# Threshold search of the 896- and 1024-key blocks begun only with group A, in smaller intervals there

## The chip, the cores and the metric

One core of a Trainium2 chip runs the program. The metric is the device time of one execution in microseconds (us). The engines are named as in the profile: PE is TensorE (PEld its weight loads), DVE VectorE, ACT ScalarE, POOL GpSimd, SP SyncE. Each has its own queue of instructions, in a fixed order.

## What is computed

One decoder layer on 1024 tokens of width 1024. Its first part, the token mixer, has two groups of heads: group A (8 heads of sparse attention, in which each query sees only the 256 keys with the highest score of a small indexer) and group B (4 heads of differential attention). Cross-attention and a gated feed-forward part follow. What matters here is the selection in group A:

```python
logits = jnp.einsum('bqhd,bsd->bqhs', qib, k_idx)
score = jnp.einsum('bqh,bqhs->bqs', wib, jax.nn.relu(logits)).astype(jnp.float32)
score = jnp.where(causal[None], score, -jnp.inf)
_, idx = lax.top_k(score, topk)            # topk = 256
...
s = jnp.where(valid[:, :, None, :], s, -jnp.inf)
p = jax.nn.softmax(s, axis=-1).astype(v.dtype)
```

## The kernel before

Tokens are tiled in eight blocks of 128 queries; by causality block i sees (i+1)*128 keys, so block 6 has 896 keys and block 7 has 1024. The stages run one after the other: the input projections with the indexer's scores (phase 0 of the search), group B (phase 1, four heads of eight units; the loop over `s` with `b_qt`, `b_s`, `b_comb`, `b_t`, `b_av`), group A (phase 2, eight blocks of eight heads; the loop with `a_t`, `a_s`, `a_av`), then the output projection of the second half, cross-attention and the feed-forward part. After block 3's last head the output projection of the first half (`wout_unit`) runs between the units of A.

The selection is not a sort. For each query row of blocks 2 to 7 a threshold is searched bit by bit, 32 iterations (`topk_iter`, L541), and then a mask is made of it (`topk_mask`, L587). Four groups of blocks are searched: blocks 2 and 3, then block 6, by ScalarE ("act"); blocks 4 and 5, then block 7, by VectorE ("dve"). An "act" iteration is one Sign with a running sum over the block's scores (L553, ScalarE) and two small VectorE instructions that make the next threshold (L555, L557); the next iteration's Sign reads that threshold. A "dve" iteration is one count (L565, VectorE) and two small instructions (L567 and L568, or L570 and L571); its first iteration has a copy on ScalarE (L562) and its sixteenth converts the scores (L580, L581). A mask is a row of VectorE instructions over the whole block (L594 to L607). Group A may not begin a block before its mask is there: `a_s` calls `topk_finish`, which issues what is still missing.

When an iteration is issued is set by hand, in virtual microseconds. After each piece of work the program calls `tick(us)`; while a queue's head is due, `us` is added to what it is owed, and whenever `PACE` of that queue is owed one iteration is issued, behind the last ScalarE and VectorE instruction of the work around it. A queue's head is due once the scores of its last block are there (`scored`). `PACE` has one pair (act, dve) for each phase:

```python
PACE = [dict(...) for x in '4,6:7,12:4,4.5'.split(':')]   # phases 0, 1, 2
```

The places of the instructions on each engine come from a scheduler that works from the program's order. Other lines that the steps below touch: in B, L774 is VectorE's masked reduction of a score row, L776 ScalarE's exp, L748 and L682 ScalarE's copies of transposed queries and probabilities, L726 VectorE's split of transposed keys, L907 a copy for the memory's keys, L797 TensorE's product with the values; in A, L1018 is the reduction, L1019 the exp, L682 the copy, L1036 the product, L1061 and L1062 ScalarE's and VectorE's part of the mixed output's split.

Of the kernel before, what the change touches and what calls it, by code (L numbers as in the profile page):

```python
# [44 lines left out]
def hybrid_layer(ctx, tc, I, out):  # L45
    nc = tc.nc
    pe, act, dve, pool, sp = nc.tensor, nc.scalar, nc.vector, nc.gpsimd, nc.sync
# [562 lines left out]
    topk_q = {"act": [], "dve": []}  # L610
# [3 lines left out]
    owed = {"act": 0.0, "dve": 0.0}  # L614
    last = {}
    scored = [1]

    PACE = [dict(zip(("act", "dve"), [float(y) for y in x.split(",")])) for x in '4,6:7,12:4,4.5'.split(':')]
    phase = [0]

    def tick(us):

        pace = PACE[phase[0]]
        for on in ("act", "dve"):
            if not topk_q[on] or topk_q[on][0][0] > scored[0]:
                continue
            owed[on] += us
            while owed[on] >= pace[on] and topk_q[on] and topk_q[on][0][0] <= scored[0]:
                owed[on] -= pace[on]
                with tc.issue_after(last["act"].ins), tc.issue_after(last["dve"].ins):  # L630
                    topk_q[on].pop(0)[1]()
# [202 lines left out]
    for c in range(2, 5):  # L834
        for t in range(NT):
            X = proj_mm(c, t)
            if c == 4 and t == 3:
                b_load_k(0)
            if c == 4 and t >= 4:
                b_k(0, (t - 4) // 2, 4 * (t % 2))  # L840
            if t == 7:
                W.free(8)
            W.pump(1 if t < 7 else 2)
            for _ in range(2):
                if idxq:
                    idxq.pop(0)()
            tick(5.2)
            if store:
                store()
            if c == 4 and t >= 6:  # L850
                b_load_q(t - 6)
            store = proj_post(c, t, X)
# [78 lines left out]
    def mem_unit(p):  # L931
        w_, c, t = mem_units.pop(0)
        X = mem_evac(t, p)
        if t == 1:
            W.free(4)
            if (w_, c) == ("xv", 1):
                W.free(2)
        if w_ == "xk":
            memk_post(c, t, X)
            mem_late.append(lambda: memk_tr(c, t, X))  # L940
        else:
            sp.dma_start(vx_d[t * P:(t + 1) * P, c * 512:(c + 1) * 512], X)
        tick(5.2)
# [6 lines left out]
    for s in range(-4, NB):  # L950
# [28 lines left out]
        if ok(s):  # L979
            b_av(s)  # L980
            W.pump(1)
            tick(0.8 + 0.85 * (i + 1))
# [753 lines left out]
```

## Time and profile before

| | us |
|---|---|
| median of 3 runs | 1676.73 (1675.79 to 1676.85) |
| profiled execution, its own time | 1677.18 |
| its span, first to last instruction | 1675.4 |
| PE busy | 1572.9 (94%) |
| DVE busy | 1222.3 (73%) |
| ACT busy | 804.1 (48%) |
| POOL busy | 641.2 (38%) |

The shares are means over stages that differ. Group B's first reduction starts at 281.1 us and group A's at 480.5; A's last block ends before 710. In these 430 us the search stands beside attention, and the rows below are taken from there. A busy share says what an engine did; what held it up is read from its waits, each put down to the instruction that came last.

### The profile page before, as it was taken

How to read it: one execution, taken by the hardware profiler on the slowest of the kernel's cores; microseconds unless marked ns; L12 is line 12 of the kernel's file. 1: busy time of each engine (PE TensorE's matmuls, PEld its weight loads, DVE VectorE, ACT ScalarE, POOL GpSimd, SP SyncE). 2: the span in 40 equal slices, each digit the busy share in tenths (PEclk: the TensorE clock that was granted, in tenths of full speed). 3: DMA queues.
4: the chain of work that ended last, by engine and by line, in shares of the span. 5: the costliest groups of instructions: out<-in, count | busy, mean ns of one | idle time of the engine just before them, and what ended most of it. 6: DMA issues, size and time to landing. Idle time of an engine off the chain costs nothing.

```text
span 1675.4 us, 22263 instructions
## 1 busy us (share of the span) xinstructions
PE 1572.9 (94%) x7596; PEld 1273.4 (76%) x7596; DVE 1222.3 (73%) x2356; ACT 804.1 (48%) x1696; POOL 641.2 (38%) x888
## 2 busy tenths in 40 slices
PE   8899987878888999999999997999999999999999
PEld 7788765666657888977777785888888777788887
DVE  5736998886778876346555369998899999865554
ACT  6545575576777445527443175432333333343432
POOL 2736656223361122031101013556666666651121
PEclk9999998989999999999999998999999999999999
DMA  8321236212120132153203021455555555799812
GB/s 283 99 83 47 77 126 212 75 51 74 49 66 27 51 101 77 45 175 115 101 1 113 26 89 63 163 170 188 177 176 178 183 187 184 253 357 379 307 51 76
DMA packets 112162, 220.06 MB, mean 131 GB/s; under 512 B 18480, under 2 KB 38448, under 8 KB 112048
## 3 DMA queue, kind: packets, MB, share of 16 engines
q1 hardware_dynamic: 91072, 148.37, 26.5%
q0 software_dynamic: 18384, 61.36, 10.3%
q10 hardware_dynamic: 2592, 8.91, 1.4%
q8 instruction: 60, 0.98, 0.2%
q14 instruction: 54, 0.44, 0.1%
HBM read 160.92 MB, written 57.67 MB: 130 GB/s over the span
## 4 chain that ended last, share of the span: by engine, by line
PE 57%; DVE 23%; DMA 7%; ACT 6%; issue 4%; POOL 3%; SPq 0%; ACTq 0%; DVEq 0%; POOLq 0%
PE acc L308 9%; PE acc L310 9%; PE acc L309 9%; PE big L309 3%; PE big L310 3%; PE big L308 3%; DVE wp L204 3%; PE acc L1036 2%; DVE jk L565 2%; PE trp L308 2%; PE trp L310 2%; PE trp L309 2%; PE trp L691 2%; DMA raw<-in_w_ffn_in_dram 2%; PE acc L885 2%
## 5 line engine op out<-in xcount | busy, mean ns | idle before, releaser
L204 DVE TENSOR_TENSOR wp<-raw,wp 128x512 fp32r<-128x512 f32 (+1 forms) x184 | 183.4, 1006 | 28.3 <-ACT wp L201 17.2
L201 ACT CAST wp<-raw 128x512 fp32r<-128x512 f32 (+1 forms) x184 | 108.4, 615 | 176.6 <-DVE raw L227 113.6
L1600 DVE TENSOR_TENSOR wp<-fo,wp 128x1024 fp32r<-128x1024 f32 x77 | 104.2, 1370 | 75.3 <-ACT wp L1599 71.6
L1549 POOL TENSOR_TENSOR fs<-fs,fs 128x512 f32<-128x512 f32 x88 | 127.6, 1450 | 63.4 <-DMA fs<-u_d 49.0
L1599 ACT CAST wp<-fo 128x1024 fp32r<-128x1024 f32 x77 | 79.8, 1049 | 107.7 <-PE big L310 46.1
L308 PE MATMUL acc<-wp,xh 128*128 128x512 f32 (+1 forms) x272 | 110.1, 407 | 10.0 <-ACT X L646 10.0
L310 PE MATMUL acc<-wp,xl 128*128 128x512 f32 (+1 forms) x272 | 109.5, 403 | 0.0
L309 PE MATMUL acc<-wp,xh 128*128 128x512 f32 (+1 forms) x272 | 109.2, 403 | 0.0
L553 ACT ACTIVATE mb<-sc,cand 128x384 bf16<-128x384 f32 (+1 forms) x96 | 75.4, 786 | 39.6 <-DVE cand L557 35.8
L203 POOL TENSOR_SCALAR wp<-raw 128x512 fp32r<-128x512 f32 (+1 forms) x36 | 24.9, 698 | 177.0 <-DVE rst L110 63.5
L682 ACT COPY pt<-trp 128x512 f32<-128x512 f32 (+3 forms) x144 | 66.3, 476 | 41.2 <-PE trp L691 40.6
L1036 PEld LDWEIGHTS acc<-va_t,pt 128*128 128x128 f32 x576 | 75.1, 196 | 9.6 <-ACT pt L682 7.6
L1036 PE MATMUL acc<-va_t,pt 128*128 128x65 f32 x576 | 77.8, 274 | 4.0 <-ACT pt L682 3.8
L1646 POOL TENSOR_TENSOR hr<-hr,r 128x512 f32<-128x512 f32 x16 | 26.8, 1686 | 115.6 <-DMA fo<-ws_d 58.4
L308 PEld LDWEIGHTS acc<-wp,xh 128*128 128x128 f32 x272 | 52.7, 194 | 23.5 <-ACT X L646 12.2
L1018 DVE CUSTOM_DVE_ANT_0 ea<-big,mb,ra 128x384 f32<-128x384 f32 (+5 forms) x48 | 45.4, 946 | 27.5 <-PE trp L691 24.4
L1497 ACT ACTIVATE fc<-fc 128x1024 f32<-128x1024 f32 x22 | 23.4, 1062 | 84.8 <-DVE fc L1496 84.8
L204 POOL TENSOR_TENSOR wp<-raw,wp 128x512 fp32r<-128x512 f32 x36 | 47.5, 1336 | 42.1 <-ACT wp L201 41.8
L774 DVE CUSTOM_DVE_ANT_0 e<-big,tri,rqk 128x1024 f32<-128x1024 f32 (+7 forms) x64 | 50.4, 812 | 16.9 <-PE big L767 14.6
L1494 ACT ACTIVATE fc<-fa,cw 128x1024 f32<-128x1024 f32 x22 | 27.4, 1245 | 71.5 <-DVE fa L1453 71.5
L1019 ACT ACTIVATE ea<-ea,sta 128x128 f32<-128x128 f32 (+7 forms) x64 | 49.5, 777 | 24.9 <-DVE sta L1018 23.0
L310 PEld LDWEIGHTS acc<-wp,xl 128*128 128x128 f32 x272 | 52.4, 193 | 11.5
(422 smaller groups left out, 5133.3 us busy)
## 6 DMA issues: line engine op xcount, KB each, us to landing
raw<-in_w_ffn_in_dram SPq DMA_DIRECT2D x44, 512.0 KB, 4.0
fs<-in_w_ffn_out_dram POOLq DMA_DIRECT2D x44, 256.0 KB, 3.5
ws_d<-fs POOLq DMA_DIRECT2D x44, 256.0 KB, 2.3
fs<-u_d POOLq DMA_DIRECT2D x44, 256.0 KB, 3.8
us_d<-fs POOLq DMA_DIRECT2D x44, 256.0 KB, 3.5
fo<-us_d SPq DMA_DIRECT2D x44, 256.0 KB, 5.4
fo<-ws_d SPq DMA_DIRECT2D x44, 256.0 KB, 5.4
u_d<-fg POOLq DMA_DIRECT2D x21, 512.0 KB, 3.7
```

The costliest lines, as they stand in the source:

```text
L201: act.copy(pg[:, 0, :n], src)
L204: (dve if el == "d" else pool).tensor_tensor(pg[:, 1, :n], src, pg[:, 0, :n].bitcast(F32), op=OP.subtract)
L308: pe.matmul(o, lhsT=lh, rhs=rh, start=start, stop=False)
L309: pe.matmul(o, lhsT=lh, rhs=rl, start=False, stop=False)
L310: pe.matmul(o, lhsT=ll, rhs=rh, start=False, stop=stop)
L553: act.activation(mb[i], sc[i], AF.Sign, bias=cf[:, j:j + 1], scale=-1.0, accum_out=cnt[:, j:j + 1])
L682: act.copy(dst, src)
L774: dve.tensor_tensor_reduce(e[:, :n], Ss[c][:, :n], tri[:, T - n:], rqk[h // 2][:, i, 2 * (h % 2) + c:2 * (h % 2) + c + 1], 3.0e38, OP.add, ...
L1036: pe.matmul(acc[:, hh * 65:hh * 65 + 65], lhsT=pt, rhs=va_t[:, kt, :], start=kt == 0, stop=kt == i)
L1549: pool.tensor_tensor(o, p, q, op=op)
L1599: act.copy(hi, raw)
L1600: dve.tensor_tensor(lo, raw, hi.bitcast(F32), op=OP.subtract)
```

## The change

In phases 0 and 1 an iteration is now due only while the queue's head belongs to a block up to 5: the searches of block 6 (act) and block 7 (dve) are not begun before group A. The intervals change too: in phase 1 that of "dve" from 12 to 10, in phase 2 from 4 and 4.5 to 2.6 and 3.2.

```diff
@@ -615,17 +615,21 @@
     last = {}
     scored = [1]
 
-    PACE = [dict(zip(("act", "dve"), [float(y) for y in x.split(",")])) for x in '4,6:7,12:4,4.5'.split(':')]
+    PACE = [dict(zip(("act", "dve"), [float(y) for y in x.split(",")])) for x in '4,6:7,10:2.6,3.2'.split(':')]
     phase = [0]
+
+    def due(on):
+
+        return bool(topk_q[on]) and topk_q[on][0][0] <= (scored[0] if phase[0] == 2 else min(scored[0], 5))
 
     def tick(us):
 
         pace = PACE[phase[0]]
         for on in ("act", "dve"):
-            if not topk_q[on] or topk_q[on][0][0] > scored[0]:
+            if not due(on):
                 continue
             owed[on] += us
-            while owed[on] >= pace[on] and topk_q[on] and topk_q[on][0][0] <= scored[0]:
+            while owed[on] >= pace[on] and due(on):
                 owed[on] -= pace[on]
                 with tc.issue_after(last["act"].ins), tc.issue_after(last["dve"].ins):
                     topk_q[on].pop(0)[1]()
```

Three places show what this moves; the added lines shift the line numbers behind L618 by four. The first is ScalarE in group B, where head 2 begins (`e` with 1024 columns is block 7's exp). Before:

```order
L776 ACTIVATE e_3254,st_3240<-e_3254,st_3240 128x1024
L553 ACTIVATE mb_940,ccnt_526<-sc_941,cand_522 128x896
L776 ACTIVATE e_3331,st_3325<-e_3331,st_3325 128x256
L907 COPY kt_3264<-trp_3259 128x512
L894 ACTIVATE sq_3269<-X_3267 128x512
L776 ACTIVATE e_3331,st_3325<-e_3331,st_3325 128x256
L798 ACTIVATE ob_2719<-acc_3097,st_3120 128x128
L748 CAST qbs_3317<-trp_3314 128x256
L553 ACTIVATE mb_940,ccnt_526<-sc_941,cand_522 128x896
L682 COPY pt_3323<-trp_3319 128x384
```

And with the change:

```order
L780 ACTIVATE e_3250,st_3236<-e_3250,st_3236 128x1024
L780 ACTIVATE e_3321,st_3315<-e_3321,st_3315 128x256
L911 COPY kt_3260<-trp_3255 128x512
L898 ACTIVATE sq_3265<-X_3263 128x512
L780 ACTIVATE e_3321,st_3315<-e_3321,st_3315 128x256
L802 ACTIVATE ob_2719<-acc_3097,st_3120 128x128
L752 CAST qbs_3307<-trp_3304 128x256
L686 COPY pt_3313<-trp_3309 128x384
```

The two Signs are gone; exp, copies and casts follow each other.

The second is ScalarE in group A, the fifth to seventh head of block 4 (640 keys). Before:

```order
L1019 ACTIVATE ea_5643<-ea_5643,sta_5490 128x640
L1061 CAST mx_5554<-trp_5556 128x512
L682 COPY pt_5576<-trp_5571 128x512
L1047 ACTIVATE sq_5798<-ob_2719 128x512
L682 COPY pt_5580<-trp_5578 128x128
L1019 ACTIVATE ea_5687<-ea_5687,sta_5490 128x640
L1061 CAST mx_5554<-trp_5595 128x512
L682 COPY pt_5632<-trp_5627 128x512
L682 COPY pt_5636<-trp_5634 128x128
L1019 ACTIVATE ea_5740<-ea_5740,sta_5490 128x640
```

And with the change:

```order
L1023 ACTIVATE ea_5633<-ea_5633,sta_5469 128x640
L1065 CAST mx_5539<-trp_5541 128x512
L686 COPY pt_5564<-trp_5559 128x512
L553 ACTIVATE mb_940,ccnt_526<-sc_941,cand_522 128x896 x3
L686 COPY pt_5568<-trp_5566 128x128
L553 ACTIVATE mb_940,ccnt_526<-sc_941,cand_522 128x896
L1023 ACTIVATE ea_5683<-ea_5683,sta_5469 128x640
L1065 CAST mx_5539<-trp_5583 128x512
L553 ACTIVATE mb_940,ccnt_526<-sc_941,cand_522 128x896
L686 COPY pt_5622<-trp_5617 128x512
L686 COPY pt_5626<-trp_5624 128x128
L1023 ACTIVATE ea_5743<-ea_5743,sta_5469 128x640
```

Where no Sign was, five stand now (one row is three in a row), each with its own pair of small instructions on VectorE. From the first exp of A to the last there are 32 now and 10 before.

The third is VectorE at the first reductions of block 5 (768 keys). Before:

```order
L1018 ISA ea_5859,sta_5853<-big_5854,mb_938,ra 128x768
L1018 ISA sta_5853 128x1
L565 TENSOR_SCALAR jk_5883,ccnt_528<-mb_942,cx_536 128x1024
L570 TENSOR_SCALAR crej_532<-ccnt_528 128x1
L571 SCALAR_TENSOR_TENSOR cx_536<-cx_536,crej_532 128x1
L1018 ISA ea_5903,sta_5853<-big_5898,mb_938,ra 128x768
L1018 ISA sta_5853 128x1
L565 TENSOR_SCALAR jk_5926,ccnt_528<-mb_942,cx_536 128x1024
L570 TENSOR_SCALAR crej_532<-ccnt_528 128x1
L571 SCALAR_TENSOR_TENSOR cx_536<-cx_536,crej_532 128x1
L1080 TENSOR_TENSOR xr_5879<-acc_5821,xr_5879 128x512
L1018 ISA ea_5947,sta_5853<-big_5942,mb_938,ra 128x768
```

And with the change:

```order
L555 TENSOR_SCALAR crej_530<-ccnt_526 128x1
L557 SCALAR_TENSOR_TENSOR cand_522<-crej_530,cand_522 128x1
L594 TENSOR_SCALAR mb_940<-sc_941,cand_522 128x896
L597 ISA jk_5851,tks<-mb_940,sc_941 128x896
L597 ISA tks 128x1
L599 TENSOR_SCALAR jk_5853,ccnt_526<-sc_941,tks 128x896
L602 TENSOR_SCALAR mb_940<-sc_941,tks 128x896
L601 TENSOR_SCALAR tks<-ccnt_526 128x1
L604 TENSOR_SCALAR jk_5857<-sc_941,tks 128x896
L1022 ISA ea_5931,sta_5877<-big_5926,mb_938,ra 128x768
L1022 ISA sta_5877 128x1
L605 SCALAR_TENSOR_TENSOR sc_941<-jk_5857 128x896
```

Counts of block 7 stood between the reductions; now the end of block 6's search and most of its mask do. The mask of block 6 stood in block 3 before, and that of block 7, in block 6 before, now stands between the fifth and the seventh reduction of block 5.

## Rows read from the trace of the kernel before

**Rows 1.** Stretches: start:end, us, busy us (count) of each engine, PEclk, DMA, GB/s.
```profile
335.60:385.60 50.00, 37.71 (x212) 30.34 (x211) 37.05 (x116) 33.96 (x84) 14.11 (x27) 0.90 0.22 64
385.60:435.80 50.20, 42.63 (x227) 31.07 (x227) 39.85 (x110) 34.22 (x83) 18.83 (x31) 0.97 0.19 58
435.80:480.50 44.70, 36.28 (x224) 29.19 (x222) 36.68 (x105) 35.94 (x90) 15.37 (x39) 0.96 0.15 46
480.50:513.70 33.20, 27.50 (x130) 21.07 (x129) 24.16 (x84) 24.23 (x61) 15.49 (x37) 0.79 0.23 72
513.70:529.00 15.30, 12.98 (x95) 10.80 (x95) 11.54 (x41) 13.44 (x30) 2.48 (x3) 1.00 0.07 19
529.00:547.00 18.00, 16.72 (x126) 14.56 (x125) 17.96 (x38) 12.71 (x24) 3.22 (x4) 1.00 0.07 23
547.00:577.20 30.20, 29.57 (x197) 26.11 (x197) 27.61 (x71) 14.39 (x26) 5.46 (x17) 1.00 0.16 49
577.20:622.00 44.80, 44.47 (x278) 38.90 (x277) 31.68 (x72) 19.57 (x35) 10.37 (x25) 1.00 0.30 101
622.00:661.50 39.50, 37.29 (x255) 33.18 (x254) 29.73 (x54) 21.49 (x35) 11.28 (x35) 1.00 0.26 87
```

**Rows 2.** Waits of TensorE in group B, 281:481: total us, times, longest.
```profile
PE trp L691 <- DVE kb L726: 9.4, 5, 3.3
...
PE acc L797 <- ACT pt L682: 6.3, 4, 3.2
```

**Rows 3.** Timeline in head 2: start us, us, engine, line, [idle before <-releaser].
```profile
340.29 1.03 ACT L553 ACTIVATE mb<-sc,cand 128x896 bf16<-128x896 f32 x1
...
341.31 0.49 ACT L776 ACTIVATE e<-e,st 128x256 f32<-128x256 f32 x1
...
341.80 0.56 ACT L907 COPY kt<-trp 128x512 f32<-128x512 f32 x1
...
342.42 0.44 PE L691 MATMUL trp<-ident,e 128*128 128x128 f32 x2 [1.43 <-ACT kt L907]
```

**Rows 4.** Groups in B, 281:481, by shape: count, busy us, mean ns, idle before.
```profile
L553 ACT ACTIVATE mb<-sc,cand 128x896 bf16<-128x896 f32 x22 | 22.9, 1042 | 7.6 <-DVE cand L557 6.4 <-DVE st L784 1.2
...
L557 DVE SCALAR_TENSOR_TENSOR cand<-crej,cand 128x1 int32<-128x1 int32 x22 | 3.9, 179 | 0.2
...
L562 ACT COPY mb<-sc 128x1024 bf16<-128x1024 bf16 x1 | 1.1, 1052 | 0.0
```

**Rows 5.** The Sign of L553 in A, 481:662, and its waits (us, times).
```profile
L553 ACT ACTIVATE mb<-sc,cand x10: 1025/1027/1042, 481.4 to 524.7; 128x896 bf16<-128x896 f32 x10
...
  DVE cand L557: 3.5, 2
```

**Rows 6.** Timeline at the end of head 4.
```profile
475.21 1.04 ACT L553 ACTIVATE mb<-sc,cand 128x896 bf16<-128x896 f32 x1 [3.98 <-DVE cand L557]
...
476.65 0.60 PE L797 MATMUL acc<-vb,pt 128*128 128x128 f32 x3 [0.64 <-ACT ob L798]
```

**Rows 7.** The chain that ended last, within 300:481, by line.
```profile
by line: PE acc L885 14.9%; DVE e L774 9.8%; PE acc L797 8.7%; ACT e L776 8.1%; PE big L767 5.2%; PE big L766 5.2%; issue 4.7%; PE trp L691 4.2%; DVE e L786 4.1%; ACT mb L553 3.6%; PE trp L723 2.9%; DVE sc L605 2.8%; ACT qbs L748 1.9%; ACT 
```

**Rows 8.** Waits of TensorE for that copy in blocks 2 to 5, 513.7:622.
```profile
PE acc L1036 <- ACT pt L682: 1.7, 4, 0.6
```

**Rows 9.** VectorE's search at the start of block 6, 622:642.
```profile
L565 DVE TENSOR_SCALAR_CACHE_REDUCE jk<-mb,cx 128x1024 bf16<-128x1024 uint16 x2 | 2.5, 1274 | 0.0
L605 DVE TENSOR_TENSOR_SCAN sc<-jk 128x1024 f32<-128x1024 bf16 x1 | 2.3, 2281 | 0.0
```

**Rows 10.** Two stretches of B at the lower clock (columns as in rows 1).
```profile
352.50:355.90 3.40, 2.88 (x14) 2.50 (x13) 3.40 (x12) 2.00 (x6) 0.77 (x3) 0.50 0.07 19
444.70:448.00 3.30, 3.30 (x15) 3.11 (x14) 3.30 (x10) 0.71 (x3) 0.31 (x1) 0.50 0.26 74
```

**Rows 11.** Waits of ScalarE for thresholds in the projections, 100:270.
```profile
ACT mb L553 <- DVE cand L557: 23.4, 16, 3.2
```

## Prediction

> **What bounds the kernel now.** I read the busy time by stretch first [rows 1]. Its first three rows are heads 2 to 4 of group B, the other six the blocks of group A: 0 and 1 together, then 2 to 6. In B no engine is full: in head 2 TensorE is busy 37.71 of 50.00 us, VectorE 37.05, ScalarE 33.96. That is a stage of waits. In A the picture turns: TensorE has 29.57 of 30.20 us in block 4 and 44.47 of 44.80 in block 5, while ScalarE has 14.39 and 19.57. In block 3 VectorE is full (17.96 of 18.00).
>
> Next the list of waits of TensorE in B [rows 2]: 9.4 us end with VectorE's split of the keys (L726), 6.3 us with ScalarE's copy of the transposed probabilities (L682), and several smaller lists end with ScalarE too. The timeline shows what such a wait is made of [rows 3]: the Sign of the search (L553) starts at 340.29, the exp behind it only at 341.31, so one iteration holds ScalarE for 1.02 us, and TensorE, which needs the copy of L907, stands for 1.43 us.
>
> **The change, part by part.** The 896-key search runs 22 of its 32 Signs in B [rows 4] and 10 in A [rows 5]; the order after the change has none in B and 32 in A. The 1024-key search moves 2 of its 32 counts and one copy (L562, 1.05 us) the same way. No DMA is added, and the sequences on SyncE and GpSimd keep their work.
>
> 1. *ScalarE in B.* In the timeline of B, eight waits of TensorE end with a ScalarE instruction that stood directly behind a Sign; the first is [rows 3], the last [rows 6]. Each gives back at most the 1.02 us of its Sign or its own length: six of them 1.02, the others 0.52 and 0.64, 7.3 us in all. The chain that ended last gives the Sign 3.6% of the 181 us of this stretch [rows 7], which is 6.5 us. I take **-7**. Ends: -7.3, and -3 if TensorE meets the next late result half the time.
>
> 2. *VectorE in B.* 22 pairs of small instructions leave, one of them 0.18 us [rows 4], and two counts of 1.28; against this the 640- and 768-key search now goes every 10 instead of 12 us, so heads 2 and 3 keep their load and head 4 is left without search. TensorE's VectorE waits lie mostly in heads 2 and 3. I take **-1**, ends 0 and -4 (half of what TensorE lacks in head 4, 44.70 less 36.28).
>
> 3. *ScalarE and VectorE in A, blocks 0 to 4.* Blocks 2 and 3 get two and six more Signs: ScalarE 13.44 + 2.0 of 15.30 us, and 12.71 + 6.1 of 18.00, so 0.2 and 0.8 us too much; VectorE in block 3, already full, gets some 2 us of counts and small instructions more than leaves it. In block 4 eleven Signs (11.2 us) fit beside 14.39 of 30.20. I take **+3**. Low end 0: in blocks 2 to 5 the copies cost TensorE only 1.7 us today [rows 8]. High end +7: the price of B, 7.3 us for 22 Signs, paid again.
>
> 4. *Block 5.* The mask of block 6 now stands between the first reductions of block 5, and the search of 1024 keys ends there and not in block 6, where it now has two counts of 1.27 us and a mask with a scan of 2.28 us and more [rows 9]. About 11 us come on top of 31.68 in 44.80 us: it fits, but in bursts. **+1**, ends 0 and +3.
>
> 5. *Block 6* loses that work; TensorE lacks 2.2 us there (39.50 less 37.29). **-1**, ends 0 and -2.
>
> Sum: -7 - 1 + 3 + 1 - 1 = **-5 us**. The profiled execution took 1677.18 us, 0.45 above the median of the runs; 1677.2 - 5 gives 1672.2, from the median 1671.7. I say **1672 us**. All low ends together give -13.3, all high ends +7.
>
> [...]
>
> **The rivals.** *A Sign that waits for its threshold blocks ScalarE in A (slower).* Each Sign needs the two small VectorE instructions of the iteration before, and VectorE is fuller in A. In blocks 0 to 4 ScalarE is idle 31.9 us [rows 1]; the moved work takes 23.5, so 8.4 us are left for such waiting. Today ten Signs in A wait 3.5 us [rows 5], 0.35 each; at that rate 22 more cost 7.7 and just fit. In the projections, at an interval of 4 too, 16 of them waited 23.4 us, 1.5 each [rows 11]. At 1.0 each, 22 us have to go into 8.4, ScalarE is 13.6 late, TensorE's copies with it, and with B's -8 the kernel is 5.6 slower: 1683. It decides from (8.4 + 8)/22 = 0.75 us a Sign. For it speaks the interval, 2.6 against 4; against it that in block 4 ScalarE is half empty and that the order puts other work between most Signs. [...]
>
> *B keeps its length (no change).* The freed copies meet VectorE: L726 waits for 9.4 us today, and the exps wait for reductions. Then point 1 is -3, point 2 nothing, A +3: 1677.
>
> *B falls to TensorE's own time where it was freed (much faster).* Head 4 loses its search on both engines and all 8.4 us of pause, heads 2 and 3 their share of point 1, 3.6 us; A costs 1: -11, 1666.
>
> **How the numbers follow.** About 0.2% (3.4 us) is what a measurement can tell from no change. My forecast (-8 to -2) has 0.42, of which a quarter lies within that band; the much faster case 0.15; no change 0.18, nearly all inside; the slower case, +3 to +14, 0.25. So faster 0.47, same 0.27, slower 0.26. The range runs from 1664, a little below the much faster case, to 1683, the slower rival's value, which leaves out some 0.06 below and 0.12 above; the forecast alone spans 1669 to 1675.
>
> **What would show it.** In B no Sign, TensorE's waits on L682, L748 and L907 down by some 7 us, and the first reduction of A (now 480.5) near 473. Blocks 0 to 4 of A (96.7 us now) 3 us longer, block 5 about 1 longer, the tail from block 7 unchanged. I am wrong on point 1 if the waits of B move to L726 and L774 and A starts after 477; wrong on point 3 if Signs in A wait over 0.75 us each or blocks 0 to 4 grow by over 7 us.

## The result and the profile after

The changed kernel is slower. Its median over 4 runs is 1687.32 us (1684.68 to 1690.14), that of the kernel before beside it 1676.26 (1675.72 to 1676.85): a ratio of 1.0063, with a 95% interval of 1.0047 to 1.0078. The profiled execution took 1686.29 us with a span of 1684.5, against 1677.18 and 1675.4 before. Of the engines TensorE alone is busy for longer (1572.9 us before); this is the first part of the page after:

```profile
PE 1578.7 (94%) x7596; PEld 1276.1 (76%) x7596; DVE 1212.8 (72%) x2356; ACT 802.8 (48%) x1696; POOL 640.8 (38%) x888
```

In the changed kernel L774 is L778, L682 is L686, L1502 is L1506.

I cut both spans at the first instruction of each stage:

| stage | before, us | after, us | difference |
|---|---|---|---|
| group B | 199.4 | 182.0 | -17.4 |
| group A, blocks 0 to 4 | 96.7 | 111.4 | +14.7 |
| block 5 | 44.8 | 49.5 | +4.7 |
| block 6 | 39.5 | 38.7 | -0.8 |
| block 7 and the output projection behind it | 157.5 | 153.1 | -4.4 |
| cross-attention | 206.3 | 206.0 | -0.3 |
| feed-forward, to the last block's convolution | 439.0 | 447.8 | +8.8 |
| the rest | 211.2 | 213.0 | +1.8 |

The projections ahead of B make up the remaining 2.0 us; among the kernels of this study they vary by -1.4 to +2.0. So B gave twice what I had forecast, A took all of it back, and some 10 us are lost from the start of the feed-forward part on, where the change has no line at all.

The stretches of the profile after, heads 2 to 4 of B, then blocks 0 and 1, 2, 3, 4, 5 and 6 of A, answer to [rows 1] and have the same columns:

```profile
335.40:376.40 41.00, 33.62 (x207) 26.09 (x206) 37.42 (x114) 27.09 (x69) 15.22 (x27) 1.00 0.25 77
376.40:425.90 49.50, 43.85 (x231) 32.83 (x230) 43.33 (x101) 28.79 (x71) 18.83 (x30) 0.93 0.19 59
425.90:465.10 39.20, 34.13 (x223) 27.62 (x222) 27.52 (x67) 27.31 (x73) 14.48 (x40) 1.00 0.17 55
...
465.10:502.60 37.50, 29.21 (x129) 22.24 (x129) 28.36 (x99) 28.36 (x68) 12.91 (x24) 0.73 0.20 66
502.60:518.90 16.30, 13.10 (x95) 11.24 (x94) 13.30 (x47) 14.02 (x30) 2.46 (x3) 0.99 0.05 12
518.90:540.90 22.00, 18.15 (x120) 15.25 (x119) 19.67 (x63) 19.93 (x41) 4.93 (x19) 0.92 0.15 47
540.90:576.50 35.60, 33.16 (x202) 29.21 (x202) 26.48 (x82) 24.52 (x46) 6.60 (x16) 0.93 0.12 39
576.50:626.00 49.50, 46.65 (x280) 40.05 (x280) 43.00 (x84) 19.98 (x38) 9.97 (x24) 0.98 0.24 81
626.00:664.70 38.70, 36.95 (x254) 32.90 (x253) 19.63 (x35) 20.93 (x35) 11.31 (x35) 1.00 0.25 89
```

Block 4 lost 5.4 us although ScalarE is busy for only 24.52 of 35.60; blocks 0 and 1, which I had not charged at all, lost 4.3. Whole stages tell more, since TensorE runs the same instructions in both kernels. First B and A of before, then B and A of after, each kernel by itself:

```profile
281.10:480.50 199.40, 157.98 (x848) 120.33 (x846) 159.12 (x452) 133.49 (x327) 64.61 (x135) 0.92 0.24 73
480.50:661.50 181.00, 168.54 (x1073) 144.61 (x1072) 142.68 (x356) 105.83 (x208) 48.30 (x120) 0.96 0.21 69
```

```profile
283.10:465.10 182.00, 151.51 (x846) 115.21 (x846) 152.12 (x401) 111.58 (x282) 65.34 (x135) 0.94 0.26 82
465.10:664.70 199.60, 177.23 (x1073) 150.88 (x1073) 150.44 (x406) 127.74 (x253) 48.20 (x120) 0.92 0.19 63
```

TensorE's own busy time is the second number. Where it changes at an equal count of instructions, they were stretched, and the granted clock moved with it (0.92 to 0.94 in B, 0.96 to 0.92 in A): the stretches granted 0.50 add up to 33.9 us in B before and 20.5 after, and to 13.7 and 30.7 in A, and half of either difference, 6.7 and 8.5, is nearly the change of the busy time, -6.5 and +8.7. What is left of the length is idle time. B: 6.5 us less busy and 10.9 less idle. A: 8.7 more busy and 9.9 more idle. So the clock is, by an estimate from these numbers, nearly four tenths of B's gain and nearly half of A's loss.

TensorE's waits in B (total us, times, longest), against [rows 2]: first two lists of before that [rows 2] leaves out, then those after the change:

```profile
PE trp L746 <- ACT qbs L748: 6.2, 6, 1.8
...
PE trp L691 <- ACT qbs L748: 1.9, 4, 0.6
```

```profile
PE trp L750 <- POOL hl L743: 8.1, 1, 8.1
PE trp L695 <- ACT qbs L752: 4.4, 6, 1.2
PE trp L750 <- ACT qbs L752: 4.2, 5, 1.1
PE acc L801 <- ACT pt L686: 3.0, 4, 1.0
...
PE trp L695 <- DVE kb L730: 2.1, 2, 1.3
```

The product's waits for the copy of the probabilities (L686) fell from 6.3 to 3.0 us, as forecast. The waits for the cast of the queries (L748, now L752) did not: with all their lists they come to 9.5 us before and 10.8 after. The three that the prediction named (L682, L748, L907) fell together from 20.2 to 16.7, by 3.5 us and not 7. The largest fall is one that I had not given to ScalarE: VectorE's split of the keys, 9.4 to 2.1. The timeline of the kernel before shows what stood behind one of its five waits (start, us, engine, line; in brackets the idle time before):

```profile
360.75 1.04 ACT L553 ACTIVATE mb<-sc,cand 128x896 bf16<-128x896 f32 x1
...
361.78 0.72 ACT L776 ACTIVATE e<-e,st 128x512 f32<-128x512 f32 x1
...
362.48 0.58 ACT L725 CAST kb<-trp 128x512 fp32r<-128x512 f32 x1
...
363.10 0.69 DVE L726 TENSOR_TENSOR kb<-trp,kb 128x512 fp32r<-128x512 f32 x1 [0.47 <-ACT kb L725]
...
363.84 0.33 PE L691 MATMUL trp<-ident,e 128*128 128x128 f32 x1 [1.79 <-DVE kb L726]
```

The wait is put down to VectorE, but VectorE had itself waited for ScalarE's cast (L725), and that cast stood behind a Sign. Three of the twelve casts of B stood within two instructions behind a Sign before, none after. Of the other four waits one, of 1.93 us at 317.9, comes before the first Sign of the 896-key search (326.6); the longest, 3.34 us at 370.59, follows a cast with five other instructions between it and the last Sign. So the step is shown for 1.79 us, and for the rest of the 7.3 us that went it is not.

TensorE's longest lists of waits in A, blocks 0 to 4, before (480.5 to 577.2) and after (465.1 to 576.5):

```profile
PE acc L1036 <- ACT pt L682: 3.5, 8, 0.9
PE big L1015 <- DVE sta L1018: 2.9, 5, 1.6
```

```profile
PE acc L1040 <- ACT pt L686: 6.5, 8, 1.7
PE big L1019 <- DVE sta L1022: 5.3, 7, 1.2
PE trp L1005 <- ACT qas L1006: 3.3, 1, 3.3
PE trp L1005 <- ACT pt L686: 1.5, 1, 1.5
```

After the change seven of the nine waits for the copy (6.9 of 8.0 us) and the one for L1006 stand within two instructions behind a Sign; before, one of eight did (0.3 of 3.5). The longest of them, in block 3:

```profile
534.96 1.02 ACT L553 ACTIVATE mb<-sc,cand 128x896 bf16<-128x896 f32 x1
...
535.98 0.56 ACT L686 COPY pt<-trp 128x512 f32<-128x512 f32 x1
...
536.60 0.66 PE L1040 MATMUL acc<-va_t,pt 128*128 128x65 f32 x4 [1.68 <-ACT pt L686]
```

And the Sign's own waits in A, against [rows 5]:

```profile
L553 ACT ACTIVATE mb<-sc,cand x32: 1025/1042/1056, 466.0 to 575.7; 128x896 bf16<-128x896 f32 x32
...
  DVE cand L557: 5.9, 10
```

Thirty-two Signs wait 5.9 us in all, 0.18 each; the ten of before had waited 0.35 each.

The third loss is in the feed-forward part. There GpSimd makes the product of a block (L1506) and, between products, loads, adds and stores the sums for the last matrix (L1549 to L1554). The chain of work that ended last, close to the end of this part (start, us, what):

```profile
1450.60 7.59 DMA fs<-u_d
...
1458.32 1.30 POOL fs L1553
...
1462.18 6.07 DMA us_d<-fs
1468.25 0.28 issue
1468.54 0.55 POOL fs L1549
...
1469.10 2.42 POOL fg L1506
1471.53 0.02 issue
1471.55 1.25 ACT fc L1498
...
1474.71 0.69 DVE fg L1457
1475.39 0.04 issue
1475.44 0.50 PE acc L308
```

Before, this stretch of the chain is TensorE alone. After, a load of the sums waits for a store of 6.07 us, the product of block 20 stands behind that load in GpSimd's queue, and ScalarE, VectorE and TensorE wait one behind the other. The last block's convolution (L1498, which the expectations below call its gelu) waited 7.06 us for that product; before, it waited 3.87 us, for VectorE. The order of GpSimd's instructions had changed here. Before, and then after (operation, out<-in, no times):

```
L1549 TENSOR_TENSOR fs<-fs,fs          L1553 TENSOR_TENSOR fs<-fs,fs
L1502 TENSOR_TENSOR fg<-fc,fg          L1554 DMA us_d<-fs
L1550 DMA us_d<-fs                     L1549 DMA fs<-u_d
L1545 DMA fs<-u_d                      L1549 DMA fs<-in_w_ffn_out
L1545 DMA fs<-in_w_ffn_out             L1506 TENSOR_TENSOR fg<-fc,fg
```

The scheduler places all instructions from one program. Another search in B and A moved rows of GpSimd, VectorE and ScalarE in a part that begins 360 us behind A's block 6: the product of block 20 by three rows here, one early product, one load in every second block, and about 28 rows of VectorE.

### The profile page after: what moved, and what is told of

Read it like the earlier page. It is cut to its first block, busy times and chain, and to the rows that moved or that the text cites. A ratio compares the mean times of both kernels' runs of the same rounds, so it can differ in the third digit from the quotient of the medians.

```text
span 1684.5 us, 22276 instructions
## 1 busy us (share of the span) xinstructions
PE 1578.7 (94%) x7596; PEld 1276.1 (76%) x7596; DVE 1212.8 (72%) x2356; ACT 802.8 (48%) x1696; POOL 640.8 (38%) x888
## 4 chain that ended last, share of the span: by engine, by line
PE 54%; DVE 22%; DMA 10%; ACT 5%; issue 5%; POOL 4%; SPq 0%; ACTq 0%; POOLq 0%; DVEq 0%
PE acc L308 9%; PE acc L309 8%; PE acc L310 8%; DVE wp L204 4%; DMA raw<-in_w_ffn_in_dram 3%; PE big L309 3%; PE big L308 3%; PE big L310 3%; DVE jk L565 3%; PE acc L889 2%; PE acc L1040 2%; DVE fc L1500 2%; PE trp L695 2%; PE big L1279 2%; PE trp L308 2%
## 5 line engine op out<-in xcount | busy, mean ns | idle before, releaser
L204 DVE TENSOR_TENSOR wp<-raw,wp 128x512 fp32r<-128x512 f32 (+1 forms) x184 | 180.8, 991 | 28.6 <-ACT wp L201 17.8
L308 PE MATMUL acc<-wp,xh 128*128 128x512 f32 (+1 forms) x272 | 111.1, 411 | 8.9 <-ACT X L650 8.9
L310 PE MATMUL acc<-wp,xl 128*128 128x512 f32 (+1 forms) x272 | 110.2, 406 | 0.0
L553 ACT ACTIVATE mb<-sc,cand 128x384 bf16<-128x384 f32 (+1 forms) x96 | 75.4, 786 | 33.6 <-DVE cand L557 30.1
L686 ACT COPY pt<-trp 128x512 f32<-128x512 f32 (+3 forms) x144 | 66.2, 475 | 47.8 <-PE trp L695 47.3
L1040 PEld LDWEIGHTS acc<-va_t,pt 128*128 128x128 f32 x576 | 76.8, 200 | 13.1 <-ACT pt L686 11.1
L308 PEld LDWEIGHTS acc<-wp,xh 128*128 128x128 f32 x272 | 53.1, 195 | 22.1 <-ACT X L650 10.7
L1501 ACT ACTIVATE fc<-fc 128x1024 f32<-128x1024 f32 x22 | 23.4, 1062 | 87.4 <-DVE fc L1500 87.4
L1498 ACT ACTIVATE fc<-fa,cw 128x1024 f32<-128x1024 f32 x22 | 27.4, 1245 | 78.8 <-DVE fa L1457 71.7
L310 PEld LDWEIGHTS acc<-wp,xl 128*128 128x128 f32 x272 | 53.1, 195 | 11.8
L309 PEld LDWEIGHTS acc<-wp,xh 128*128 128x128 f32 x272 | 53.3, 196 | 11.5
L889 PE MATMUL acc<-wp,wp 128*128 128x512 f32 x128 | 58.8, 604 | 0.0
```

Source lines behind the costliest of these rows:

```text
L204: (dve if el == "d" else pool).tensor_tensor(pg[:, 1, :n], src, pg[:, 0, :n].bitcast(F32), op=OP.subtract)
L308: pe.matmul(o, lhsT=lh, rhs=rh, start=start, stop=False)
L309: pe.matmul(o, lhsT=lh, rhs=rl, start=False, stop=False)
L310: pe.matmul(o, lhsT=ll, rhs=rh, start=False, stop=stop)
L553: act.activation(mb[i], sc[i], AF.Sign, bias=cf[:, j:j + 1], scale=-1.0, accum_out=cnt[:, j:j + 1])
L686: act.copy(dst, src)
```

## The experiments

Two theories stood after the result. *T*: the loss at the end comes from the order behind A, which is a by-product. *S*: the search itself, crowded into A, costs the 10 us. Intervals are given as in the code, act and dve of phase 2; "deferral" is the new function `due`. All runs, with the lengths that the verdicts rest on (from the profiled executions; "A" is blocks 0 to 6, "end" from the start of the feed-forward part to the end). The runs were taken in four rounds, each with the kernel before beside it (medians 1676.26 for the change, then 1674.58 for the e runs, 1675.12 for f, 1674.35 for g and n), so the ratios compare, and not the medians:

| kernel | median, us | ratio to before | B | A | end |
|---|---|---|---|---|---|
| before, 4 and 4.5 | | 1 | 199.4 | 181.0 | 650.2 |
| the change, 2.6 and 3.2 | 1687.32 | 1.0063 (1.0047 to 1.0078) | 182.0 | 199.6 | 660.7 |
| e1, 2.6 and 3.3 | 1674.36 | 0.9994 (0.9979 to 1.0010) | 183.9 | 197.5 | 648.6 |
| e2, before with 3.9 | 1680.60 | 1.0046 (1.0029 to 1.0062) | 196.9 | 182.5 | 653.6 |
| e3, 3.7 and 4.5 | 1662.80 | 0.9929 (0.9910 to 0.9949) | 179.5 | 186.2 | 649.6 |
| e4, no deferral, 2.6 and 3.2 | 1681.39 | 1.0037 (1.0023 to 1.0050) | 192.9 | 192.4 | 647.3 |
| f1, 4 and 4.5, phase 1 at 12 | 1679.33 | 1.0030 (1.0015 to 1.0045) | 184.9 | 191.5 | 659.2 |
| f2, 3.7 and 4.5, phase 1 at 12 | 1684.20 | 1.0059 (1.0037 to 1.0082) | 184.1 | 194.7 | 656.3 |
| f3, 2.6 and 4.5 | 1679.22 | 1.0033 (1.0016 to 1.0051) | 183.6 | 193.5 | 658.0 |
| f4, 3.7 and 3.3 | 1666.29 | 0.9945 (0.9924 to 0.9966) | 183.0 | 187.8 | 647.8 |
| g1, the change, one product moved | 1680.72 | 1.0039 (1.0022 to 1.0056) | 180.4 | 198.8 | 653.5 |
| g2, e3, one product moved | 1663.40 | 0.9941 (0.9919 to 0.9962) | 180.5 | 186.5 | 647.2 |
| n1, 3.7 and 4.0 | 1661.49 | 0.9924 (0.9905 to 0.9943) | 180.1 | 185.9 | 648.6 |
| n2, 3.9 and 4.5 | 1669.29 | 0.9978 (0.9963 to 0.9993) | 180.7 | 193.9 | 648.3 |

**The smallest step away from the change (e1).** One interval by 0.1 us; behind A all instructions stand in the order of before.

```diff
-'4,6:7,10:2.6,3.2'
+'4,6:7,10:2.6,3.3'
```

> The change with one number different: the dve interval in group A is 3.3 instead of 3.2. The search stands in A as in the change (32 Signs there, none in B), but behind A every instruction of VectorE, ScalarE, GpSimd and SyncE stands in the order of the kernel before. Theory T (the change loses its time in the feed-forward stage, because the scheduler put GpSimd's products and loads in another order there): A's end about 3 us later than before, cross-attention level, and the whole 1675 to 1679 us. Theory S (the search in A itself costs the 10 us): 1685 to 1690 us.

It took 1674.36 us, no different from before, and 0.7% less than the change by the two ratios. B and A are 0.2 us shorter together than in the change, the end 12.1. *T* held.

**The order without the deferral (e2).** The kernel before with one interval changed by 0.1 us. The same ten Signs run in A, but behind A the order is the change's.

```diff
-'4,6:7,12:4,4.5'
+'4,6:7,12:3.9,4.5'
```

> The kernel before with one number different: the act interval in group A is 3.9 instead of 4. Search in B and A as before, but behind A the order of the change on VectorE, ScalarE, GpSimd and SyncE. Theory T: 1683 to 1688 us, lost between the first feed-forward block and its end (8 to 12 us). Theory S: 1675 to 1678 us, nothing lost.

1680.60 us, 0.46% slower, with a search that is the same to the eye: less than *T* named, but on its side. Its profiled execution ran faster than its median and lost only 3.4 us at the end, but it has the late convolution of the change: 22.9 us behind the one before it (19.4 before), then a wait of TensorE of 3.4 us for the sum (L1457).

**The deferral with wide intervals (e3).**

```diff
-'4,6:7,10:2.6,3.2'
+'4,6:7,10:3.7,4.5'
```

> The change with wider intervals in group A: act 3.7, dve 4.5. Nothing of blocks 6 and 7 is searched in B, the Signs reach into block 5, and behind A the order is that of the kernel before. Theory T with the reading that A's 18 us are the crowding of Signs in blocks 0 to 4: B keeps its 15 us, blocks 0 to 4 cost 8 instead of 15, the whole 1666 to 1673 us. If A's cost does not depend on the interval: 1675 to 1679 us.

1662.80 us, 0.7% faster than before. B keeps its whole gain (-19.9) and A gives back 5.2, where the change gave back 18.6. So the idea of the change pays; its intervals and the order that came with them do not.

**The intervals without the deferral (e4).**

```diff
-        return bool(topk_q[on]) and topk_q[on][0][0] <= (scored[0] if phase[0] == 2 else min(scored[0], 5))
+        return bool(topk_q[on]) and topk_q[on][0][0] <= scored[0]
```

> The intervals of the change (10 in B; 2.6 and 3.2 in A) without the deferral: blocks 6 and 7 are begun in B as before. GpSimd and SyncE in the order of the kernel before behind A. Theory T: 22 Signs stay in B, so B keeps its length; A is a little denser at its start and free of search earlier: 1674 to 1679 us. If the short intervals are what hurts A: 1680 us or more.

1681.39, slower, with the end in the order of before (647.3). The rival held: A loses 11.4 us with no more Signs than before (ten; the counts of the 1024-key search in blocks 0 to 4 are 28 instead of 20), and B gains only 6.5. Short intervals cost A by themselves. In B TensorE's idle time is 38.7 us here, 41.4 before and 30.1 to 32.1 in every kernel with the deferral, f1 with the intervals of before among them: the 10 us of waits go with the deferral, and the rest of B's gain is TensorE's busy time (6.5 us in the change and 9.1 in n1, at a clock of 0.94 and 0.96 against 0.92). The split of the keys is not the measure of it: its waits are 4.7 us here, with all 22 Signs still in B, and 4.4 in f1, which has none. *S* is therefore right about A and wrong about the end: both losses are real.

**The deferral alone, and e3 with another phase 1 (f1, f2).** First f1, then f2:

```diff
-'4,6:7,10:2.6,3.2'
+'4,6:7,12:4,4.5'
```

```diff
-'4,6:7,10:2.6,3.2'
+'4,6:7,12:3.7,4.5'
```

> The change's deferral alone, with the intervals of before (4 and 4.5 us in A). Its order of GpSimd and VectorE in the feed-forward stage is that of the change, not that of before. Theory O (that order costs the 6 us by which the run with a 3.9 us interval and the old search was slower; the search itself is cheap at wide intervals): A begins 15 to 20 us earlier, block 7 begins 10 to 16 us earlier than before, and the time is 1665 to 1670. Rival N (the order costs nothing by itself): the time is 1660 to 1664, as in the run with 3.7 and 4.5 us, which differs by its order too.

> The deferral with 3.7 and 4.5 us in A, as in the best run so far, but with the middle stage's VectorE interval at 12 us as before, not 10. A's search is the same as in that run; behind A the feed-forward stage is in the change's order, not that of before. Theory O: marks up to block 7 within 2 us of that run's, and a time 5 to 9 us over it, 1667 to 1672. Rival N: the time is that run's within 2 us, 1661 to 1665.

1679.33 and 1684.20: both slower than either theory had them. The end took 659.2 and 656.3 us, so *O* was right there (6 to 9 us). f1's block 7 began only 3.1 us ahead of before, not 10 to 16: its block 5 takes 58.2 us (44.8 before), with 11 Signs and 10 counts of the search left for it. And f2's block 7 began 0.2 us after that of before, not 15 us ahead as in e3. My expectation that its A would be that of e3 was wrong: the VectorE interval of B moved instructions of B and A too. Both have the same 32 Signs in A's blocks 0 to 5 and nearly the same counts, yet A is 8.5 us longer in f2. Of that, 8.0 is TensorE's busy time (175.45 against 167.49 us, at a clock of 0.92 against 0.98), 0.5 its pauses. Why the same search loses the clock in one order and keeps it in the other is open.

**Which engine's interval costs in A (f3, f4).** Against e3 one interval is short: ScalarE's in f3 (the first diff), VectorE's in f4.

```diff
-'4,6:7,10:3.7,4.5'
+'4,6:7,10:2.6,4.5'
```

```diff
-'4,6:7,10:3.7,4.5'
+'4,6:7,10:3.7,3.3'
```

> The deferral with the change's ScalarE interval (2.6 us) and the VectorE interval of before (4.5 us); feed-forward stage in the change's order. Read by the start of block 7 against before, at +3.2 us in the change and -15.0 us with 3.7 and 4.5 us. Theory V (VectorE's short interval is what costs A): -10 to -15 us, and a time of 1666 to 1672. Rival A (ScalarE's short interval, whose Signs stand between a block's evictions, is what costs): -3 to +3 us, and a time of 1678 to 1684. Both share: about -6 us, 1674.

> The deferral with 3.7 us for ScalarE and 3.3 us for VectorE (the change has 2.6 and 3.2 us); feed-forward stage in the order of before. The run with 2.6 and 3.3 us took 1674.4 with block 7 at +1.1 us, that with 3.7 and 4.5 us took 1662.8 with block 7 at -15.0 us. Theory V: block 7 at -3 to +2 us and 1672 to 1676. Rival A: block 7 at -10 to -15 us and 1663 to 1667. Both share: about -6 us, 1669.

f3's block 7 began 3.0 us ahead of before, f4's 10.9; e3's was at -15.0. By this mark ScalarE's short interval costs 12 us and VectorE's 4, and together they make the 16 of e1, which has both short (+1.1): rival A, nearly as it was put. Two things keep it from being shown. Of the 12 us 7.3 lie in A and 4.1 in B, of the 4 us 1.6 in A and 3.5 in B. And f2, with e3's wide intervals in A, is 15.2 us behind e3 at the same mark: another order alone does as much. What does part the kernels is TensorE's idle time in blocks 0 to 4: 15.9 to 19.2 us in the five with 2.6 (the change, e1, e4, f3, g1), 11.1 to 15.1 in the seven that have the deferral and 3.7 or more. So ScalarE's short interval costs waits; what it costs in clock is not settled. In time f4 took 1666.29. f3 took 1679.22, but its end is in the change's order and 8.4 us longer than e3's.

**One instruction moved (g1).** The change, with GpSimd's load of the sums held behind the product of block 20 (`prod[0]`), so that this product stands two rows earlier. All other rows, on all engines, are where the change has them.

```diff
+                if m == NM - 2:
+                    with tc.issue_after(prod[0]):
+                        x["12"] = ld(1, 0)
+                    return
                 x["12"] = ld(1, 0)
```

> The change with one instruction in another place: GpSimd's product of feed-forward block 20 (L1506) stands two rows earlier, ahead of the load of the sums (L1549) that waits for a store; every other row on every engine is where it was. Theory O (that place costs the stretch before the last gelu, and a pause behind it that lowers TensorE's clock): the last block's gelu comes 19.5 to 21 us after the one before it instead of 22.6, no half-clock stretch at 1476, the time falls by 3 to 7 us, to 1680 to 1684. Rival N (the product's place is covered): under 1.5 us, 1686 or more.

1680.72 us. GpSimd's timeline there, with the product now ahead of both loads:

```profile
1458.08 0.56 POOL L1554 DMA_DIRECT2D us_d<-fs  x1 [0.30 <-POOL fs L1553]
1458.66 2.55 POOL L1506 TENSOR_TENSOR fg<-fc,fg 128x1024 f32<-128x1024 f32 x1
1461.16 0.59 POOL L1549 DMA_DIRECT2D fs<-u_d  x1
1462.35 0.55 POOL L1549 DMA_DIRECT2D fs<-in_w_ffn_out_dram  x1 [0.60 <-DMA us_d<-fs]
```

The last convolution comes 19.2 us behind the one before it, not 22.6, and TensorE's wait of 3.1 us for the sum behind it (L1457) is gone. *O* held there. The half-clock stretch did not go: one of 3.40 us, granted 0.50, begins at 1478.4 instead of 1475.8, behind two waits of 1.3 and 0.8 us for split weights (L1607, L1608) in the next stage, which is 3.3 us longer than after the change. By the ratios the move gives 0.24%, 4 us; the two intervals still overlap a little. The rest of the feed-forward loss of the change's profile lies earlier in it, in part in a half-clock stretch of 3.4 us at 1305 that no other profile of this study has. I don't count that one as shown.

**The same instruction moved the other way (g2).** e3, with that product and its store (`prod`) behind the load; `then` is set for the load of the fourth sum.

```diff
-            pool.tensor_tensor(g, cv, g, op=OP.mult)
-            pool.dma_start(u_d[f * P:(f + 1) * P, :], g)
+            late.append(prod) if f == FT - 2 else prod()
...
-            pool.dma_start(t, src(m, odd, half))
+            d = pool.dma_start(t, src(m, odd, half))
+            if then and m == NM - 2:
+                with tc.issue_after(d.ins):
+                    late.pop()()
```

> The other way round: the best run so far (3.7 and 4.5 us, 1662.8) with that one product two rows later, behind the load, as the change has it; one other load of the end stands three rows earlier, all other rows are the same. Theory O: the last block's gelu comes 22.5 to 24 us after the one before it instead of 20.9, a half-clock stretch follows, and the time rises by 3 to 7 us to 1666 to 1670. Rival N: within 1.5 us of 1662.8.

One other load of the end stands three rows earlier. 1663.40, no loss: rival N. In this kernel the load waited only 0.28 us, and the product behind it started at 1443.0 (1443.5 in e3). So the place alone is not the price. It cost in the change, where GpSimd came late to the loads ahead of the product and they waited 0.66 and 2.34 us. That the rows moved in the first blocks are what makes GpSimd late in the change is argued only; they were not tried alone.

**Neighbours of the best (n1, n2).** First n1, then n2:

```diff
-'4,6:7,10:3.7,4.5'
+'4,6:7,10:3.7,4.0'
```

```diff
-'4,6:7,10:3.7,4.5'
+'4,6:7,10:3.9,4.5'
```

> Neighbour of the best run: 3.7 us for ScalarE, 4.0 us for VectorE in A (4.5 there, 3.3 in the run at 1666.3). If VectorE's interval costs steadily, block 7 begins 11 to 15 us earlier than before and the time is 1663 to 1666. If the best run was one lucky order, it lies outside, at 1668 or more.

> Neighbour of the best run: 3.9 us for ScalarE, 4.5 us for VectorE in A (3.7 there). If wider intervals are steadily better or equal, block 7 begins 13 to 17 us earlier than before and the time is 1660 to 1665. If the best run was one lucky order, 1668 or more.

n1 has the lowest median of the study, 1661.49 us, 0.76% under before, and is no different from e3 and g2. n2 misses: 1669.29, with block 5 at 60.4 us (44.8 before, 54.1 in e3) and 10 Signs and 10 counts left for it (9 and 8 in e3). By the expectation that was the mark of one lucky order in e3; n1 and f4, which keep most of its gain, speak against it, so the gain is not that one order's, but it does not grow with the interval. B and A of n1:

```profile
280.80:460.90 180.10, 148.91 (x846) 112.48 (x846) 152.43 (x401) 111.19 (x282) 65.35 (x135) 0.96 0.26 81
460.90:646.80 185.90, 170.36 (x1072) 144.86 (x1072) 148.28 (x405) 127.68 (x253) 51.84 (x120) 0.96 0.20 67
```

The moved Signs and counts are all there. A's busy time is 1.8 us over that of before, and its idle time 15.5 against 12.5.

## Why the prediction was wrong

1. *ScalarE in B, -7, and VectorE in B, -1.* The direction was right, the size half of what came: -17.4. The waits that point 1 summed were not what paid: TensorE's waits for the three ScalarE lines that it named fell by 3.5 us. The eight waits were said to stand directly behind a Sign; in four of them one or two exps stand between. The waits put down to VectorE's split of the keys, on which the sum had nothing, fell by 7.3; one of them hung on a Sign through one more step, the cast at L725, and why the others fell is open. That -7 lies near 7.3 is luck. The other 6.5 us are TensorE's busy time, by the estimate above through its clock. The sum had no term for that: the two stretches of [rows 10] are 6.7 us at 0.50, and B had 33.9 us of such stretches before and 20.5 after.
2. *Blocks 0 to 4 of A, +3 (0 to +7).* +14.7, twice the 7 us that the prediction set as its mark of being wrong: the term that failed first. I compared busy sums with lengths, block by block, and charged only what did not fit. But TensorE waits for single copies and reductions, and in the rows above most of the copies that it waits for stand close behind a Sign of 1.02 us, even in block 4 with ScalarE busy for 24.52 of 35.60 us. Idle time of TensorE went from 9.9 to 17.8 us there (lengths less busy time, from [rows 1] and the rows above), busy time from 86.8 to 93.6, with 13.7 us granted 0.50 before and 29.1 after. The high end, "the price of B paid again", was 7.3 for 22 Signs. The whole of A paid 18.6, about what B really got back, 17.4; that is no rule, since in e3 the same search cost A 5.2. e4 and the idle times above show that the short intervals cost A; how the 14.7 divide between ScalarE's and VectorE's is not shown.
3. *Block 5, +1 (0 to +3)*: +4.7. *Block 6, -1*: -0.8, right. Block 7 with the projection behind it gave 4.4 us that I had not named; in the other kernels it gave 0.6 to 3.6, and why is not settled.
4. *"The tail from block 7 unchanged", "the sequences on SyncE and GpSimd keep their work".* They keep their work, not their order. This is the step that turned a level result into a slower one: e1, with nearly the change's B and A, is level with before, and e2, with nearly before's B and A, is slower by 0.46%. In all five profiles with the change's order behind A the end takes 653.6 to 660.7 us, in the seven with the order of before (before itself, e1, e3, e4, f4, n1, n2; in the last four of them a few rows of VectorE and ScalarE differ) 647.3 to 650.2. In the same five the last convolution comes 22.6 to 23.7 us behind the one before it, TensorE then waits 3.1 to 4.2 us, and a stretch at 0.50, of 3.4 or 6.8 us, begins within that wait or just behind it; in the seven it comes 19.3 to 20.9 us behind, and no such stretch follows. That the order costs the end is shown by this; which of its moved rows cost what lies beyond the late product is not.
5. *The slower rival* gave the right sign by the wrong mechanism. Its decision point was 0.75 us of waiting per Sign; it is 0.18. Its value, 1683, is only by chance close to the result. The result itself lies 4 us above my range: nothing in it stood for an order that changes elsewhere.
6. *TensorE's clock* stood in no term of the sum. TensorE's busy time fell by 6.5 us in B (0.92 to 0.94) and rose by 8.7 in A (0.96 to 0.92).

## What to carry to other kernels

When work is moved out of a stage of waits, follow each wait one step further back than the list names it, and price the stage that takes the work by the same waits, not by its free busy time: it can pay what the other saved. After any edit of a scheduled program, compare the order of every engine over the whole program, also in stages that the edit does not touch, and look there for an instruction that now stands behind a wait for a DMA. An interval set by hand should be tried at its neighbours: a tenth of a microsecond here moved the time by 0.5 to 0.7%, through the order behind A and not through the search itself.

## What the runs showed of the hardware

TensorE's clock moved nearly as much time as its waits did: 6.5 us in B beside 10.9, 8.7 in A beside 9.9, with no wait over 3.3 us in A's blocks 0 to 4. One stretch behind the late product of the change, in which TensorE is busy throughout, shows it by itself:

```profile
1475.80:1479.20 3.40, 3.40 (x10) 2.62 (x9) 2.22 (x3) 1.06 (x1) 1.83 (x2) 0.50 0.74 213
```

It is granted 0.50, right behind the wait of 3.1 us that the chain ended with. In it TensorE's products (L308 to L310, 128x512) start 0.43 us apart, behind it 0.23: an estimate from these numbers is 1.6 us lost of the 3.4. The other four kernels with such a wait (e2, f1, f2, f3: 3.4 to 4.2 us) have a stretch at 0.50 there too, of 3.4 or 6.8 us; g1 has one of 3.40 us behind its waits of 1.3 and 0.8 us, and e3, which waits 1.6 us, has none. What brings such a stretch on is not shown. Second, GpSimd's product stood behind loads that GpSimd issues itself: at 1465.65 and 1468.54 the two loads of the sums waited 0.66 and 2.34 us for a store, and the product behind them started at 1469.10, 20.2 us behind the convolution of the block before, although ScalarE's part of its input (L1501) was finished at 1454.45; in g1, ahead of them, it started 16.6 us behind.
